# Group 0's output projection and first norm in one range of 512 tokens, with gMLP's last gate unit and two head units behind them

## The chip, the core and the metric

The kernel runs on one core of a Trainium2 chip. Its engines work side by side, each through its own queue in order: TensorE (PE, matmuls; its weight loads are PEld), VectorE (DVE), ScalarE (ACT), GpSimd (POOL) and SyncE (SP), which here issues nearly all DMAs. The metric is the device time of one execution in microseconds (us), as the median of several runs. Where several kernels are compared, less is better.

## The reference

One layer of a streaming encoder, for a prompt of 1024 tokens and a sample of 32 tokens of a running stream, with the same weights (`D_MODEL` 1024, `D_FF` 2816, all in float32):

```python
sh1, sc1, g1, sh2, sc2, g2 = jnp.split((jax.nn.silu(c) @ w_ada + b_ada)[:, None, :], 6, axis=-1)
h = x * (1 + sc1) + sh1
mq, mk, mv, mo, mi, mf, fq, fk, fv, ff, gu, gv = jnp.split(h @ w_in, split_at, axis=-1)
hm = ...   # mLSTM, chunk by chunk
hf = ...   # forgetting attention (FoX), causal
vn = _layer_norm(gv, gmlp_ln_g, gmlp_ln_b)
hg = _spatial_gate(gu, vn, gmlp_ws, gmlp_bs)      # gMLP, in chunks of 128 tokens
mix = jnp.concatenate([hm, hf, hg], axis=-1) @ w_o
x = _layer_norm(ALPHA * x + (1 + g1) * mix, ln1_g, ln1_b)
h = x * (1 + sc2) + sh2
y = (jax.nn.silu(h @ w_gate) * (h @ w_up)) @ w_down
x = _layer_norm(ALPHA * x + (1 + g2) * y, ln2_g, ln2_b)
```

## The kernel before

**Layout.** Features lie on the 128 partitions (KT = 8 blocks of 128), tokens along the free dimension. The 1056 tokens are two groups: group 0 is tokens 0 to 511, group 1 the other 512 and the 32 of the sample (544). Tokens are also counted in 9 tiles: 0 to 3 are group 0, 4 to 7 and the sample tile 8 are group 1. `MM[0]` cuts group 0 into ranges of 256 tokens, `MM[1]` group 1 into ranges of 272; `WIDE` is group 0 in one range of 512.

**Products.** Each float32 product is made of three matmuls of rounded parts (`gemm`, L117 to L119): an operand x is split into a high part (a cast, on ScalarE) and the rest (a subtraction, on VectorE). `weights` loads a weight block of 512 KB into one of three buffers (`raw`), casts it (L105) and splits it (L106). An operand's buffers are `hh` and `hl`.

**Order.** The program is written in an order, but each instruction is placed by a scheduler that simulates the engines; the queues that result are fixed. Memory pools are stacks: a pool that is opened gets the room of one that was closed, and what is written into it waits for the last readers of the old tiles.

**The stage of the change**, in the order in which it is written in `run`:

- The mixers of group 0, `fox` (heads q0 to q7) and `mlstm` (four chunks), with high priority; in their pauses other units' matmuls run. Their outputs go to HBM (`dmix[0]`, eight blocks of 128 rows).
- `wo_res(0)` loads the residual x into `z[0]` (8 loads of 256 KB); `wo_mix(0, ...)` brings `dmix[0]` back, a block and a range of 256 tokens at a time, through four buffers `tmp`, and splits it (L919, L920): first blocks 2, 3, 4, 5, 0, 1 (`KORDER[:6]`) for the one range, then for the other; blocks 6 and 7 (gMLP's) at its second call.
- Four gMLP units (`tm_unit`): 0 and 2 make `gv` with its norm (`evac_gv`) for tiles 0 to 3 and 4 to 8, 1 and 3 make `gu` and the gate (`evac_gmlp`) for the same tiles. A tile is 24 matmuls (L282 to L284, for the sample tile L287 to L290); `evac_gmlp` adds a load of `gvn`, a copy on ScalarE (L644), eight small products (L649), four VectorE operations (L652), transposes (L631), a copy (L633) and a store to `dmix`.
- `fm_unit` for heads 2 and 3, group 1 only: 48 matmuls each; evacuation on ScalarE (L366), VectorE (L367) and GpSimd (L368, into `o_kT`), with three stores per range.
- `wo(0, ...)` for the first and then for the second range of 256: for each of 8 output blocks m it loads `w_o[m]`, makes 24 matmuls, adds the residual (L960), subtracts a pivot (L955, GpSimd; the pivot is the mean of block 0), and sums z (L860, GpSimd) and its squares (L856, L862). For m = 0 the matmuls go by operand block, as these arrive.
- `ln1(0, ...)` for each range: means by matmuls with ones (L872), reciprocal root (L879 to L883), then for each block a multiplication (L977), an addition (L978, for two of eight blocks on GpSimd), an affine step on ScalarE (L981) and the split (L985, L986) into the buffers that the projection's operand had.
- `fm_unit` for heads 4 to 7, and `ln1_res(0)`, GpSimd's 16 operations on z (L995).
- The mixers of group 1, at high priority, over the SwiGLU units `up(0, j)` and `down(0, g)` of group 0. Unit j = 0 runs in two ranges of 256, the others in one of 512; behind each of the first four stands one conditioning unit (`ada`, L179).

PSUM has eight banks; `pg`, from which the gMLP units, heads and the projection take theirs, has three of them.

Of the kernel before, what the change touches and what calls it, by code (L numbers as in the profile page):

```python
# [7 lines left out]
F32 = mybir.dt.float32  # L8
F32R = mybir.dt.float32r
AF = mybir.ActivationFunctionType  # L10
ALU = mybir.AluOpType
# [58 lines left out]
class Kernel:  # L70
# [769 lines left out]

    def ln_pivot(self, st, z, sl):
        nc = self.nc
        ps = self.t(self.pt, [P, 512], F32, "t")
        n = sl.stop - sl.start
        nc.tensor.matmul(ps[:, :n], self.ones8, z[:, 0, sl], start=True, stop=True)
        nc.scalar.copy(st["pv"][:, sl], ps[:, :n])
        nc.vector.tensor_tensor(z[:, 0, sl], z[:, 0, sl], st["pv"][:, sl], ALU.subtract)

    def ln_sum(self, st, z, m, sl):
# [5 lines left out]
        sq = self.t(self.p2, [P, 272], F32, "tmp", 4)[:, :sl.stop - sl.start]  # L855
# [29 lines left out]
    def ln_stats(self, st, sl):  # L885
# [3 lines left out]
        v = self.t(self.p2, [P, 272], F32, "tmp", 4)[:, :sl.stop - sl.start]  # L889
# [61 lines left out]
    def sublayer_end(self, c, z, m, ps, gate, st, a, b):  # L951
# [3 lines left out]
        less = lambda: self.nc.gpsimd.tensor_tensor(z[:, m, sl], z[:, m, sl], st["pv"][:, sl], ALU.subtract)  # L955
# [13 lines left out]
    def ln1(self, c, st, a, b):  # L969
# [3 lines left out]
        for k in range(KT):  # L973
# [4 lines left out]
            (nc.gpsimd if k % 4 == 1 else nc.vector).tensor_tensor(zk, zk, e, ALU.add)  # L978
            h = self.t(self.p2, [P, 272], F32, "tmp", 4)[:, :b - a]
# [250 lines left out]
    def run(self):  # L1230
# [114 lines left out]
        for i in range(4):  # L1345
            if i == ADAPOS:
                tail_ada()
            self.tm_unit(w2[3 + i % 2], 256, (self.evac_gv, self.evac_gmlp)[i % 2], range(4 * (i // 2), 4 + i // 2 * 5),
                         nc.gpsimd if GENG[i] else nc.vector)
        if ADAPOS == 4:  # L1350
            tail_ada()
        for h in range(QD, PRE):
            self.fm_unit(w3[2 + h], self.evac_qk(h), (1,))
        s6.close()
        self.wo_mix(0, self.KORDER[6:])
        self.pn = self.pool("pn")
        self.ln_consts()
        st = self.ln_begin(nc.gpsimd)
        for cut in MM[0]:
            self.wo(0, st, (cut,), nc.vector)  # L1360
        self.operand(0, self.ph)
        for a, b in MM[0]:
            weave(self.ln1(0, st, a, b))
        for h in range(PRE, 8):
            self.fm_unit(w3[2 + h], self.evac_qk(h), (1,))
        self.ln1_res(0)
# [10 lines left out]
        for g, (j0, nj) in enumerate(GROUPS):  # L1377
# [26 lines left out]
            for j in range(j0 + (g > 0), j0 + nj + (g < last)):  # L1404
                weave(self.up(0, j, act, pa, WIDE if 0 < j < GROUPS[-1][0] else MM[0]))
                if j < 4:
                    self.ada(20 + j, self.wp, "raw", RAW, self.pg, "g")
# [165 lines left out]
```

## Time and profile before

| | |
|---|---|
| median of 3 runs | 1400.97 us (1399.07 to 1403.76) |
| span of the profiled execution, first to last instruction | 1388.5 us |
| between the span and the median of the runs | 12.5 us |
| PE / DVE / ACT / POOL busy | 97% / 74% / 46% / 19% |
| mean granted TensorE clock | 0.993 |

The time of the profiled execution itself is not among the runs; its span is what the stage rows add up to. Where a row shows an engine's instructions, its name is followed by the source line (L106), the operation, and output and inputs by the program's names. A tile's name begins with the phase in which it was made: `tm_` belongs to the gMLP units, `fm_` to heads, `wo_` to the projection, `lna_` to the first norm, `up_` to the SwiGLU units. `mlstm_ah` and `mlstm_al` are the operand buffers `hh[0]` and `hl[0]`, and `mlstm_z` is `z[0]`. A matmul's duration reaches past the start of the next one; its cost in a stream is the distance from start to start.

### The profile page before, as it was taken

The page shows a single profiled execution, that of the slowest core. Times are in us where ns is not written, and L with a number is a line of the kernel's source. Part 1 is how long each engine was busy: PE and PEld are TensorE (multiplying, and loading weights), DVE is VectorE, ACT ScalarE, POOL GpSimd, SP SyncE. Part 2 cuts the span into 40 slices and gives each one's busy share as a digit, 9 for nine tenths or more (in the row PEclk, how much of TensorE's full clock was granted, in tenths as well). Part 3 has the DMA queues.
Part 4 walks back from the last instruction along what each step waited for, and adds up shares of the span by engine and source line. Part 5 has one row for each costly group of instructions (what it writes and reads, how often), then busy time and mean ns, then how long its engine had stood idle before and what let it go on. Part 6 is the DMA issues. An engine that isn't in the chain of part 4 may idle for free.

```text
span 1388.5 us, 25995 instructions
## 1 busy us (share of the span) xinstructions
PE 1345.2 (97%) x9683; PEld 1236.4 (89%) x9683; DVE 1034.2 (74%) x2214; ACT 641.3 (46%) x1261; POOL 259.1 (19%) x292
## 2 busy tenths in 40 slices
PE   7999999999999799999999999999999999999996
PEld 4899988899899778888887889899999999999996
DVE  5548656678689657777776766677898988888777
ACT  3323234444455444545544445335574544545355
POOL 0103200052157500000000000264610000000341
PEclk9999999999999899999999999999999999999998
DMA  9754577575665665444443442664497767453321
GB/s 362 266 211 134 176 242 212 187 237 149 212 205 160 180 184 182 125 131 137 133 135 86 108 127 81 195 169 134 157 229 195 216 163 214 136 175 115 101 90 65
DMA packets 136373, 233.09 MB, mean 168 GB/s; under 512 B 22564, under 2 KB 79532, under 8 KB 136248
## 3 DMA queue, kind: packets, MB, share of 16 engines
q1 hardware_dynamic: 130936, 221.34, 50.7%
q0 software_dynamic: 5168, 9.96, 4.7%
q8 instruction: 76, 1.25, 0.4%
q14 instruction: 49, 0.40, 0.1%
q10 hardware_dynamic: 144, 0.14, 0.0%
HBM read 197.50 MB, written 53.81 MB: 181 GB/s over the span
## 4 chain that ended last, share of the span: by engine, by line
PE 67%; DVE 5%; DMA 3%; ACT 1%; issue 1%; SPq 0%; POOL 0%; DVEq 0%; ACTq 0%
PE up_g L117 5%; PE up_g L118 5%; PE up_g L119 5%; PE dn_g L119 4%; PE dn_g L117 4%; PE dn_g L118 4%; PE sup_u L119 3%; PE sup_u L117 3%; PE sup_u L118 3%; PE wo_g L119 2%; PE wo_g L117 2%; PE wo_g L118 2%; PE sup_g L118 2%; PE sup_g L119 2%; PE sup_g L117 2%; PE fox_t L738 2%
## 5 line engine op out<-in xcount | busy, mean ns | idle before, releaser
L117 PE MATMUL up_g<-mlstm_ah,up_whi 128*128 128x512 f32 (+1 forms) x384 | 141.7, 369 | 4.4 <-ACT lna_tmp L981 3.3
L118 PE MATMUL up_g<-mlstm_al,up_whi 128*128 128x512 f32 (+1 forms) x384 | 142.1, 370 | 0.4 <-DVE mlstm_al L986 0.4
L119 PE MATMUL up_g<-mlstm_ah,up_wlo 128*128 128x512 f32 (+1 forms) x384 | 141.1, 368 | 0.0
L282 PE MATMUL tm_g<-tm_whi,start_h1h 128*128 128x256 f32 (+1 forms) x384 | 109.7, 287 | 1.5 <-ACT tm_mixs L633 1.5
L284 PE MATMUL tm_g<-tm_whi,start_h1l 128*128 128x256 f32 (+1 forms) x384 | 109.6, 287 | 0.0
L283 PE MATMUL tm_g<-tm_wlo,start_h1h 128*128 128x256 f32 (+1 forms) x384 | 109.5, 286 | 0.0
L117 PE MATMUL fm_g<-start_h1h,fm_whi 128*128 128x256 f32 (+2 forms) x344 | 101.7, 301 | 6.1 <-DVE fm_qkl L367 2.6
L118 PE MATMUL fm_g<-start_h1l,fm_whi 128*128 128x256 f32 (+2 forms) x344 | 100.8, 293 | 0.0
L119 PE MATMUL fm_g<-start_h1h,fm_wlo 128*128 128x256 f32 (+2 forms) x344 | 100.0, 292 | 0.0
L1105 ACT CAST sup_whi<-sup_raw 128x1024 fp32r<-128x1024 f32 x54 | 56.0, 1048 | 91.5 <-PE dn_u L118 47.9
L117 PEld LDWEIGHTS up_g<-mlstm_ah,up_whi 128*128 128x128 f32 x384 | 73.5, 192 | 16.7 <-ACT mlstm_ah L985 3.5
L118 PEld LDWEIGHTS up_g<-mlstm_al,up_whi 128*128 128x128 f32 x384 | 73.7, 192 | 12.3 <-DVE mlstm_al L986 1.5
L119 PEld LDWEIGHTS up_g<-mlstm_ah,up_wlo 128*128 128x128 f32 x384 | 73.8, 192 | 10.6
L105 ACT CAST up_whi<-up_raw 128x1024 fp32r<-128x1024 f32 x50 | 52.4, 1048 | 63.9 <-PE dn_g L118 25.1
L711 ACT ACTIVATE fox_p<-fox_s,fox_fmx 128x384 f32<-128x384 f32 (+2 forms) x96 | 55.0, 578 | 57.1 <-DVE fox_fmx L709 44.0
L282 PEld LDWEIGHTS tm_g<-tm_whi,start_h1h 128*128 128x128 f32 x384 | 72.2, 189 | 4.4 <-ACT tm_mixs L633 2.1
L117 PEld LDWEIGHTS fm_g<-start_h1h,fm_whi 128*128 128x128 f32 x344 | 64.7, 190 | 12.5 <-DVE fm_qkl L367 3.5
L1106 DVE TENSOR_TENSOR sup_wlo<-sup_raw,sup_whi 128x1024 fp32r<-128x1024 f32 x54 | 67.8, 1259 | 10.5 <-ACT sup_whi L1105 10.5
L106 DVE TENSOR_TENSOR up_wlo<-up_raw,up_whi 128x1024 fp32r<-128x1024 f32 x50 | 66.8, 1336 | 10.4 <-ACT up_whi L105 9.6
L284 PEld LDWEIGHTS tm_g<-tm_whi,start_h1l 128*128 128x128 f32 x384 | 72.2, 188 | 1.5 <-issue 1.2
L117 PE MATMUL dn_g<-up_acth,dn_whi 128*128 128x512 f32 (+2 forms) x200 | 73.5, 368 | 0.0
L118 PE MATMUL dn_g<-up_actl,dn_whi 128*128 128x512 f32 (+2 forms) x200 | 73.3, 368 | 0.0
(591 smaller groups left out, 4594.5 us busy)
## 6 DMA issues: line engine op xcount, KB each, us to landing
up_raw<-w_gu SPq DMA_DIRECT2D x50, 512.0 KB
dn_raw<-w_dn SPq DMA_DIRECT2D x28, 512.0 KB
ada_late<-w_ada SPq DMA_DIRECT2D x24, 512.0 KB
wo_raw<-w_o SPq DMA_DIRECT2D x24, 512.0 KB
sup_raw<-w_gu SPq DMA_DIRECT2D x20, 512.0 KB
start_dp<-w_gu SPq DMA_DIRECT2D x19, 512.0 KB
start_dp<-w_gu POOLq DMA_DIRECT2D x19, 512.0 KB, 7.8
sup_raw<-start_dp SPq DMA_DIRECT2D x18, 512.0 KB
```

The source lines that it names most:

```text
L105: nc.scalar.copy(hi[:, :w], raw[:, :w])
L106: (eng or nc.vector).tensor_tensor(lo[:, :w], raw[:, :w], f(hi[:, :w]), ALU.subtract)
L117: nc.tensor.matmul(ps, hi, xh(k), start=start and k == 0, stop=False)
L118: nc.tensor.matmul(ps, hi, xl(k), start=False, stop=False)
L119: nc.tensor.matmul(ps, lo, xh(k), start=False, stop=stop and k == n - 1)
L282: nc.tensor.matmul(ps[:, :ncol], xh, hi, start=k == 0, stop=False)
L283: nc.tensor.matmul(ps[:, :ncol], xh, lo, start=False, stop=False)
L284: nc.tensor.matmul(ps[:, :ncol], xl, hi, start=False, stop=k == 7)
L711: nc.scalar.activation(pr[:, lo:hi], banks[x][:, :hi - lo], AF.Exp, bias=mxs[:, 0:1], accum_out=sums[:, x:x + 1])
L738: nc.tensor.transpose(ps[:, c:c + P], probs[y][:, b * P:(b + 1) * P], self.ident)
L1105: nc.scalar.copy(h, x)
L1106: tt(l, x, f(h), ALU.subtract)
```

## The change

Group 0's projection takes one range of 512 tokens, so w_o is loaded and split once, in place of twice. In this range the pivot's subtraction and the sum of z go to VectorE (`st["eng"]` is `nc.vector`; group 1 keeps GpSimd), and so do the two additions of the norm that GpSimd had. Buffers of 512 columns come from a pool `pw` (`ltmp`). gMLP's unit 3 and heads 2 and 3 are written behind the norm. The conditioning units 20 to 23 go from the first SwiGLU units to heads 4 to 7, and SwiGLU unit 0 takes one range of 512. `wo_mix` still loads by ranges of 256.

```diff
+    def ltmp(self, n):
+        if n > 272:
+            return self.t(self.pw, [P, 512], F32, "wide", 4)[:, :n]
+        return self.t(self.p2, [P, 272], F32, "tmp", 4)[:, :n]
...
-        sq = self.t(self.p2, [P, 272], F32, "tmp", 4)[:, :sl.stop - sl.start]
+        sq = self.ltmp(sl.stop - sl.start)
...
-        v = self.t(self.p2, [P, 272], F32, "tmp", 4)[:, :sl.stop - sl.start]
+        v = self.ltmp(sl.stop - sl.start)
...
-        less = lambda: self.nc.gpsimd.tensor_tensor(z[:, m, sl], z[:, m, sl], st["pv"][:, sl], ALU.subtract)
+        less = lambda: (self.nc.gpsimd if c else st["eng"]).tensor_tensor(z[:, m, sl], z[:, m, sl], st["pv"][:, sl],
+                                                                          ALU.subtract)
...
-            (nc.gpsimd if k % 4 == 1 else nc.vector).tensor_tensor(zk, zk, e, ALU.add)
-            h = self.t(self.p2, [P, 272], F32, "tmp", 4)[:, :b - a]
+            (nc.gpsimd if c and k % 4 == 1 else nc.vector).tensor_tensor(zk, zk, e, ALU.add)
+            h = self.ltmp(b - a)
...
-        for i in range(4):
-            if i == ADAPOS:
-                tail_ada()
-            self.tm_unit(w2[3 + i % 2], 256, (self.evac_gv, self.evac_gmlp)[i % 2], range(4 * (i // 2), 4 + i // 2 * 5),
-                         nc.gpsimd if GENG[i] else nc.vector)
-        if ADAPOS == 4:
-            tail_ada()
-        for h in range(QD, PRE):
-            self.fm_unit(w3[2 + h], self.evac_qk(h), (1,))
+        gate = lambda i: self.tm_unit(w2[3 + i % 2], 256, (self.evac_gv, self.evac_gmlp)[i % 2],
+                                      range(4 * (i // 2), 4 + i // 2 * 5), nc.gpsimd if GENG[i] else nc.vector)
+        for i in range(3):
+            gate(i)
+        tail_ada()
         s6.close()
         self.wo_mix(0, self.KORDER[6:])
         self.pn = self.pool("pn")
+        sw = ExitStack()
+        self.pw = self.pool("pw", ctx=sw)
         self.ln_consts()
-        st = self.ln_begin(nc.gpsimd)
-        for cut in MM[0]:
-            self.wo(0, st, (cut,), nc.vector)
-        self.operand(0, self.ph)
-        for a, b in MM[0]:
-            weave(self.ln1(0, st, a, b))
-        for h in range(PRE, 8):
+        st = self.ln_begin(nc.vector)
+        self.wo(0, st, WIDE, nc.vector)
+        weave(self.ln1(0, st, *WIDE[0]))
+        gate(3)
+        for h in range(QD, 8):
             self.fm_unit(w3[2 + h], self.evac_qk(h), (1,))
+            if h >= PRE:
+                self.ada(16 + h, self.wp, "raw", RAW, self.pg, "g")
+        sw.close()
         self.ln1_res(0)
...
-                weave(self.up(0, j, act, pa, WIDE if 0 < j < GROUPS[-1][0] else MM[0]))
-                if j < 4:
-                    self.ada(20 + j, self.wp, "raw", RAW, self.pg, "g")
+                weave(self.up(0, j, act, pa, WIDE if j < GROUPS[-1][0] else MM[0]))
```

## The prediction

> **What bounds the kernel now.** I read the page first, then busy time by stage, then the waits of the stage that the change touches, then single instructions there.
>
> ```profile
> span 1388.5 us, 25995 instructions
> PE 1345.2 (97%) x9683; PEld 1236.4 (89%) x9683; DVE 1034.2 (74%) x2214; ACT 641.3 (46%) x1261; POOL 259.1 (19%) x292
> 346.90:361.50 14.60, 14.60 (x129) 13.39 (x127) 13.69 (x48) 5.62 (x14) 5.11 (x4) 1.00 0.38 113
> 361.50:384.70 23.20, 20.87 (x169) 19.87 (x168) 13.03 (x34) 11.61 (x27) 1.93 (x3) 1.00 0.86 269
> 384.70:433.80 49.10, 47.37 (x392) 46.88 (x391) 42.67 (x53) 24.54 (x39) 33.04 (x30) 1.00 0.63 197
> 433.80:461.10 27.30, 26.38 (x201) 25.52 (x200) 21.77 (x42) 15.78 (x34) 16.57 (x19) 1.00 0.48 149
> 461.10:488.00 26.90, 20.55 (x129) 18.21 (x130) 20.80 (x53) 12.83 (x30) 12.76 (x19) 0.81 0.72 197
> 482.00:536.00 54.00, 53.66 (x340) 41.55 (x340) 32.03 (x79) 26.57 (x58) 0.95 (x1) 0.99 0.65 192
> 536.00:700.00 164.00, 164.00 (x854) 137.89 (x851) 126.97 (x275) 81.55 (x163) 4.56 (x9) 1.00 0.47 140
> ```
>
> Columns of the stage rows: stretch, length, then busy time of TensorE matmul, TensorE weight load, VectorE, ScalarE, GpSimd, then granted clock. TensorE sets the end (97%); from 482 on it never pauses, so what it loses or gains before that reaches the end one for one. The prediction is a ledger of TensorE's lost time between 346.9 and the SwiGLU units at 461-488.
>
> Losses now: 0 + 2.33 + 1.73 + 0.92 + 6.35 = 11.3 us. The 6.35 are mostly the norm and a bank that is late, and the clock halves behind those pauses:
>
> ```profile
> PE up_g L117 <- ACT lna_tmp L981: 3.3, 1, 3.3
> PE ada_g L179 <- DVE up_sil L1037: 2.3, 1, 2.3
> 465.00:470.00 5.00, 2.08 (x18) 1.87 (x16) 5.00 (x11) 3.68 (x8) 2.61 (x3) 0.93 0.17 60
> 470.00:475.00 5.00, 4.22 (x18) 3.96 (x19) 2.90 (x8) 5.00 (x14) 5.00 (x9) 0.50 0.48 146
> 475.00:480.00 5.00, 2.69 (x26) 1.90 (x25) 3.89 (x10) 0.61 (x2) 2.11 (x5) 0.84 0.88 217
> 480.00:485.00 5.00, 5.00 (x36) 4.45 (x28) 2.40 (x8) 0.95 (x2) 0.00 (x0) 0.71 1.16 246
> ```
>
> At half clock half the busy time is lost: 4.22/2 in the second row, about 0.75 in the third (1.6 us halved), 1.45 in the fourth (2.9 us halved): 4.3 us. Before: 15.6 us in all. That is the most that a better cover of the norm can return.
>
> **What the change saves in matmuls.** The projection goes from 384 matmuls of 256 columns to 192 of 512. Start to start:
>
> ```profile
> 462.26 0.28 PE L117 MATMUL up_g<-mlstm_ah,up_whi 128*128 128x256 f32 x1
> 462.38 0.28 PE L118 MATMUL up_g<-mlstm_al,up_whi 128*128 128x256 f32 x1
> 560.98 0.39 PE L118 MATMUL up_g<-mlstm_al,up_whi 128*128 128x512 f32 x1
> 561.21 0.39 PE L119 MATMUL up_g<-mlstm_ah,up_wlo 128*128 128x512 f32 x1
> ```
>
> 0.12 against 0.23 us (0.119 and 0.2335 over longer runs): 45.7 against 44.8 us, 0.9 saved; unit 0's 96 into 48 save another 0.2. Half of the weight loads, casts and splits of w_o fall away (8 each); they already run beside matmuls, so nothing. The four conditioning units (ada) that go from the first SwiGLU units into heads 4 to 7 are the same matmuls elsewhere; their loads share three weight buffers with the heads, whose 6 us of matmuls cover a load of 2.1, its cast and its split (1.2, L106 below): nothing.
>
> **What it uncovers ahead of the projection.** Up to the last matmul of gate unit 2 both instruction orders are alike. Behind it TensorE now runs gate unit 3 and heads 2 and 3; in the changed order only the remains of the mixers stand there, then the projection. The projection cannot start then. Its operand comes through HBM, issued in order on SP's queue:
>
> ```profile
> 346.76 0.28 PE L288 MATMUL tm_g<-tm_whi,start_hs 128*64 128x256 f32 x1
> 359.55 0.43 DVE L621 TENSOR_TENSOR mlstm_mhm<-mlstm_mhm,mlstm_mo 128x256 f32<-128x256 f32 x1
> 360.96 0.38 SPq L91 DMA_DIRECT2D start_dmix<-mlstm_mixs  x1
> 362.56 3.75 SPq L87 DMA_DIRECT2D mlstm_z<-xT  x8
> 366.35 2.37 SPq L87 DMA_DIRECT2D wo_tmp<-start_dmix  x4
> 372.46 2.41 SPq L87 DMA_DIRECT2D wo_tmp<-start_dmix  x4
> 371.57 1.50 ACT L919 CAST mlstm_ah<-wo_tmp 128x256 fp32r<-128x256 f32 x4 [1.20 <-DMA wo_tmp<-start_dmix]
> 379.63 1.75 SPq L87 DMA_DIRECT2D wo_tmp<-start_dmix  x4
> 382.28 0.41 ACT L919 CAST mlstm_ah<-wo_tmp 128x256 fp32r<-128x256 f32 x1 [0.16 <-DMA wo_tmp<-start_dmix]
> ```
>
> The mixers' last store leaves at 361. It follows L621, and the stretch 346.9-361.5 has VectorE busy 13.69 of 14.60: VectorE sets it. In the changed order VectorE has the same work there (two weight splits of w_o replace the two of gate and head), so I leave the store at 361. Behind it on SP, as now, come eight loads of x (2 MB) and the 16 loads of the mixers' output through four buffers; the first casts come 9.0 us after the first x load (362.56 to 371.57). With nothing between, later groups of four need a free buffer (cast 0.4, split 0.4), issue and landing: 2.1 us uncontended (379.63 to 381.7), some 3.1 in all. Loading still goes by 256-token halves, but a 512-wide matmul needs both, and the first row block of the second half is load 7: cast at 375.5. Bounds: 372.5 if every landing is short; 378.5 if the second group lands as late as today (372.46 to 378.74).
>
> Gate 3's and the heads' own loads and stores, which today stand among these on SP, are behind them now; that is already in the 3.1.
>
> ```profile
> 346.90:384.70 37.80, 20.32 (x164) 18.62 (x162) 5.53 (x23) 3.78 (x11) 1.00 0.68 209
> 346.90:384.70 37.80, 12.63 (x95) 12.16 (x96) 1.00 (x2) 1.45 (x3) 1.00 0.68 209
> ```
>
> These are the same stretch for the gate's matmuls (tm_g) and the heads' (fm_g) alone: 20.3 + 12.6 = 33 us with overlapping ends, some 31.5 without. 35.5 us were busy there in all, so 4.0 of mixer work stay. 346.9 to 375.5 is 28.6 us; lost: **24.6 us** (21.6 to 27.6). This is the term that decides.
>
> After it the projection runs behind at half clock, as after the pause at 467-470 (6.8 us halved there): I take 2.0 us (0 to 3.4), since part of it coincides with waiting for the last loads.
>
> [...]
>
> **What the norm does to its new cover.** Behind the projection stand gate unit 3, heads 2 to 7: 31.5 + 24 us of TensorE work, longer than the norm. But gate 3's evacuation is on VectorE too (L652), queued between the norm's instructions, and TensorE has three PSUM banks. Durations:
>
> ```profile
> L554 DVE TENSOR_TENSOR mlstm_mw<-mlstm_s,mlstm_mw x9: 269/691/692, 264.9 to 759.0; 128x512 f32<-128x512 f32 x8, 32x128 f32<-32x128 f32 x1
> L977 DVE TENSOR_TENSOR mlstm_z<-mlstm_z,wo_pv x16: 410/414/970, 440.8 to 466.4; 128x256 f32<-128x256 f32 x16
> L106 DVE TENSOR_TENSOR wo_wlo<-wo_raw,wo_whi x24: 1203/1226/2097, 370.6 to 934.5; 128x1024 fp32r<-128x1024 f32 x24
> L652 DVE SCALAR_TENSOR_TENSOR tm_traw<-tm_g,start_colp,tm_traw x36: 262/274/285, 314.2 to 375.9; 128x64 f32<-128x64 f32 x32, 32x64 f32<-32x64 f32 x4
> L872 PE MATMUL lna_t<-wo_zs,start_onesm x8: 377/384/392, 433.6 to 974.7; 128*128 128x256 f32 x4, 128*128 128x272 f32 x4
> L649 PE MATMUL tm_g<-tm_gvn,start_wsp x72: 214/275/281, 313.1 to 375.0; 128*128 128x64 f32 x64, 32*32 32x64 f32 x8
> L960 DVE SCALAR_TENSOR_TENSOR mlstm_z<-dn_g,start_mod,mlstm_z x48: 467/750/755, 541.8 to 997.2; 128x512 f32<-128x512 f32 x40, 128x256 f32<-128x256 f32 x8
> L862 DVE TENSOR_TENSOR wo_qs<-wo_qs,wo_tmp x28: 428/954/2120, 401.3 to 953.6; 128x256 f32<-128x256 f32 x14, 128x272 f32<-128x272 f32 x14
> ```
>
> A 512-wide VectorE operation lies between the 256- and the 1024-wide rows, near L554: 0.69 busy, 0.60 start to start as neighbours overlap. Within the projection VectorE needs 0.75 + 1.2 + 2 x 0.6 = 3.2 us for a block of 5.6 us matmuls: hidden, and no longer doubled by GpSimd (L862: 0.43 to 2.12). The seven pivot subtractions that it takes from GpSimd come in one piece behind the first block, 4.2 us, while two more blocks are being multiplied: hidden too; without that cover they would hold the next bank for 4.2 us.
>
> From the projection's end (0), down both queues. VectorE: last block, sum, a weight split, sum of squares, 3.1. TensorE takes the two means between gate matmuls, 0.43 for each 256 columns (two L872 that overlap), and is through with them at 7.6. Variance 8.3, logarithm and exponential on ScalarE 9.7, three VectorE steps to the reciprocal root 11.6, half of the second tile's L652 and the shift 13.3, eight multiplications 18.1, the other half 18.6. TensorE has by then 96 matmuls (11.4), the means (1.7), one pair of transposes (0.25) and three times eight small products (2.5; L649 at 0.1 start to start) behind it, and wants that tile's transposes at 15.9: 2.7 lost. It goes on with the sample tile (24 matmuls, 2.9) and 1.1 of products and transposes, and at 22.8 wants those of the fourth tile, all banks full; its L652 stand on VectorE behind the third tile's, eight additions, three operand splits and a weight split: 28.6, 5.8 lost. **8.5 us** (0 if the evacuations get through as they do today; 12.5 if GpSimd's ln1_res, which runs beside the additions, slows VectorE as in L862's upper half). Another pause, another half clock: 1.5 us (0 to 3.4). The last splits end at some 35 us, before the heads do; the SwiGLU units find their operand ready, so the two waits at 461-488 go.
>
> **Sum.** After: 24.6 + 2.0 + 8.5 + 1.5 = 36.6. Before: 15.6. Matmuls -1.1. 36.6 - 15.6 - 1.1 = **+19.9 us**: span 1408.4. The runs lie at 1400.97 where the profiled span is 1388.5, 12.5 outside it; the forecast is **1421**. Extremes: 21.6 - 16.7 = +5; 27.6 + 3.4 + 12.5 + 3.4 - 16.7 = +30. Its own range 1412 to 1428.
>
> **Rivals.**
> 1. *Only the hole ahead of the projection.* VectorE serves gate 3 in time. For it: today VectorE is busy only 21.77 of 27.30 in 433-461. Against it: an in-order queue with eight operations ahead of L652. 24.6 + 2.0 - 16.7 = +10: 1411.
> 2. *Not slower: TensorE's own queue holds the mixers' tail.* Of the 14.60 us busy in 346.9-361.5, 10.6 are filler that stands ahead of the mixers' matmuls. If that made the tail late, dropping it brings the store, and all of SP's chain, 10.6 us forward; the hole shrinks to 14.0, and with the evacuations in time and the clock kept: 14.0 - 16.7 = -3: 1398. It decides from a first projection matmul before 367.6. Against it: VectorE's 13.69 of 14.60, and 9 us of loads that stay.
> 3. *Worse behind the norm.* GpSimd has all 16 ln1_res ahead of the first head's o_kT addition, whose stores stand on SP ahead of later weight loads.
>
> ```profile
> L995 POOL TENSOR_SCALAR mlstm_z<-mlstm_z,start_colp x16: 550/822/1768, 445.8 to 476.6; 128x256 f32<-128x256 f32 x16
> ```
>
>  If the second eight take 1.77 us each instead of 0.55, the heads wait some 10 us more: +30, 1431.
> 4. That the change does nothing is excluded by the built order: 8735 rows of TensorE instructions against 8977, and the moved units behind the norm.
>
> **Chances.** Forecast 0.56, rival 1 0.20, rival 2 0.08, rival 3 0.13, rest 0.03. 1407 to 1431 takes in rivals 1 and 3 and leaves out rival 2. No change that can be told here means within 0.3% (4.2 us): rival 2 mostly falls there or just below. Faster 0.05, same 0.06, slower 0.89.
>
> **What would show it.** Right: TensorE idle for some 14 us without break up to about 375, released by a cast of the mixers' output; the projection ending some 10 us earlier than 433.8 all the same; two pauses of 3 and 6 us ahead of gate 3's transposes, released by its L652 on VectorE; granted clock 0.5 behind each; no wait for the norm at the first SwiGLU unit. Wrong: a mixers' store well before 361, a first projection matmul before 368, or no VectorE-released pauses behind the projection.

## The result and the profile after

| | before | after |
|---|---|---|
| median of 4 runs | 1400.64 us (1399.07 to 1403.76) | 1433.05 us (1431.06 to 1434.53) |
| ratio, 95% interval | | 1.0247 (1.0225 to 1.027) |
| span of the profiled execution | 1388.5 us | 1429.0 us, in a run of 1431.06 |

The change costs 32.4 us. The forecast was 1421, its range ended at 1431. Slower was right, and so was the hole in which most of the time goes; 12 us more were lost than the sum had.

The stages of the kernel after: stretch, length, busy time of TensorE matmul, TensorE weight load, VectorE, ScalarE, GpSimd, then granted clock.

```profile
span 1429.0 us, 25316 instructions
PE 1355.0 (95%) x9437; PEld 1232.4 (86%) x9437; DVE 1022.2 (72%) x2176; ACT 628.9 (44%) x1221; POOL 225.1 (16%) x260
...
354.63:383.30 28.67, 6.00 (x39) 3.42 (x37) 14.99 (x51) 7.58 (x19) 5.05 (x4) 0.61 0.52 167
383.30:388.40 5.10, 5.09 (x12) 4.03 (x13) 2.74 (x7) 2.43 (x6) 0.00 (x0) 0.50 0.60 175
388.40:431.40 43.00, 43.00 (x184) 34.28 (x184) 26.99 (x38) 13.43 (x19) 0.00 (x0) 1.00 0.29 88
431.40:508.60 77.20, 67.20 (x525) 61.11 (x523) 39.54 (x83) 28.70 (x53) 28.60 (x32) 0.93 0.47 146
508.60:538.60 30.00, 28.98 (x139) 22.86 (x142) 19.03 (x33) 13.52 (x20) 2.44 (x6) 1.00 0.82 232
540.00:800.00 260.00, 260.00 (x1347) 217.48 (x1346) 184.75 (x394) 124.67 (x249) 4.76 (x11) 1.00 0.46 125
800.00:820.00 20.00, 17.86 (x77) 13.70 (x76) 13.85 (x26) 9.04 (x20) 0.72 (x1) 0.91 0.49 112
820.00:925.00 105.00, 105.00 (x601) 90.00 (x600) 75.32 (x155) 49.83 (x102) 0.00 (x0) 1.00 0.39 104
925.00:955.00 30.00, 26.11 (x185) 24.33 (x184) 20.82 (x30) 12.81 (x31) 16.91 (x15) 0.94 0.64 199
```

The first row begins behind the last matmul of gate unit 2 and ends with the projection's first: 28.67 us, of which TensorE works 6.00. The second is the projection's beginning at half clock, the fourth gate unit 3 and the heads behind the norm. The two rows behind 800 are new: in the kernel before, TensorE lost 0.7 us between 540 us and the end of group 1's projection.

What TensorE waited for in the kernel after (total, times, longest) between 340 and 560 us:

```profile
PE wo_g L117 <- ACT mlstm_ah L924: 14.2, 1, 14.2
PE tm_g L631 <- DVE tm_traw L652: 6.1, 2, 3.4
PE mlstm_t L631 <- DVE mlstm_mhm L621: 6.0, 1, 6.0
PE mlstm_t L560 <- DVE fox_ptl L744: 1.7, 1, 1.7
...
PE fm_g L119 <- DVE fm_wlo L106: 1.0, 2, 0.7
PE tm_g L288 <- ACT tm_mixs L633: 1.0, 1, 1.0
PE up_g L117 <- ACT up_whi L105: 1.0, 1, 1.0
PE fm_g L117 <- ACT fm_whi L105: 0.9, 1, 0.9
```

The same view between 560 and 1000 us, whole:

```profile
PE fox_s L702 <- ACT fox_p L711: 2.1, 1, 2.1
PE wo_g L117 <- ACT up_ah L924: 2.0, 2, 1.7
PE wo_g L118 <- DVE up_al L925: 1.4, 2, 0.8
PE wo_g L117 <- DMA wo_raw<-w_o: 0.5, 1, 0.5
```

The first hole is three waits in a row (1.7, 6.0, 14.2). The second view holds two more holes. Its first row is a wait of the mixers themselves, at 801.6: TensorE wants the next scores of `fox`, ScalarE is late with an exponential (L711), and that stands in ScalarE's queue behind a gate of the mLSTM (L538), which waited for its load:

```profile
801.23 0.42 ACT L538 ACTIVATE mlstm_mo<-mlstm_mo 32x256 f32<-32x256 f32 x1 [6.41 <-DMA mlstm_mo<-start_dmo]
```

In the kernel before, the same operation waited 4.76 us, and TensorE 0.5. The other three rows are the second hole proper, with `up_ah` and `up_al` the operand of *group 1's* projection. Its cause shows in one view: the last matmuls of the mixers of group 1 (L751) and the first of group 1's projection (L117), with count, durations, first and last start. First the kernel before, then after:

```profile
L751 PE MATMUL fox_o<-fox_pth,fox_v x112: 272/280/287, 530.0 to 874.8; 128*128 128x256 f32 x96, 128*128 128x128 f32 x16
L117 PE MATMUL wo_g<-up_ah,wo_whi x128: 282/287/487, 901.8 to 950.4; 128*128 128x272 f32 x128
```

```profile
L751 PE MATMUL fox_o<-fox_pth,fox_v x112: 272/280/288, 573.8 to 924.9; 128*128 128x256 f32 x96, 128*128 128x128 f32 x16
L117 PE MATMUL wo_g<-up_ah,wo_whi x128: 282/287/486, 935.6 to 991.1; 128*128 128x272 f32 x128
```

Between the two lay 27.0 us of SwiGLU matmuls; now there are 10.7. In these the last mixer output must be stored, loaded and split, and that takes longer. In the order as built, 160 SwiGLU matmuls stood there and now 84. (These matmuls of the mixers begin 44 us later and end 50 us later, the projection begins 34 us later.)

### The profile page after: what moved, and what is told of

The parts are those of the page before. It is cut to its first block, busy times and chain, and to the rows that moved or that the text cites. A ratio compares the mean times of both kernels' runs of the same rounds, so it can differ in the third digit from the quotient of the medians.

```text
span 1429.0 us, 25316 instructions
## 1 busy us (share of the span) xinstructions
PE 1355.0 (95%) x9437; PEld 1232.4 (86%) x9437; DVE 1022.2 (72%) x2176; ACT 628.9 (44%) x1221; POOL 225.1 (16%) x260
## 4 chain that ended last, share of the span: by engine, by line
PE 60%; DVE 7%; DMA 5%; issue 3%; ACT 1%; SPq 0%; POOL 0%; DVEq 0%; ACTq 0%; POOLq 0%
PE up_g L117 5%; PE up_g L118 5%; PE up_g L119 5%; PE dn_g L119 3%; PE dn_g L117 3%; PE dn_g L118 3%; PE sup_u L119 3%; PE sup_u L117 3%; PE sup_u L118 3%; PE wo_g L117 2%; PE wo_g L118 2%; PE wo_g L119 2%; PE sup_g L119 2%; PE sup_g L118 2%; PE sup_g L117 2%
## 5 line engine op out<-in xcount | busy, mean ns | idle before, releaser
L117 PE MATMUL up_g<-mlstm_ah,up_whi 128*128 128x512 f32 (+1 forms) x368 | 138.0, 375 | 1.0 <-ACT up_whi L105 1.0
L119 PE MATMUL up_g<-mlstm_ah,up_wlo 128*128 128x512 f32 (+1 forms) x368 | 137.6, 374 | 0.5 <-DVE up_wlo L106 0.5
L118 PE MATMUL up_g<-mlstm_al,up_whi 128*128 128x512 f32 (+1 forms) x368 | 137.2, 373 | 0.0
L117 PE MATMUL fm_g<-start_h1h,fm_whi 128*128 128x256 f32 (+2 forms) x344 | 102.6, 303 | 6.8 <-ACT fm_whi L105 2.8
L117 PEld LDWEIGHTS up_g<-mlstm_ah,up_whi 128*128 128x128 f32 x368 | 69.2, 188 | 13.3 <-ACT up_whi L105 1.4
L119 PEld LDWEIGHTS up_g<-mlstm_ah,up_wlo 128*128 128x128 f32 x368 | 69.2, 188 | 12.9 <-DVE up_wlo L106 1.0
L711 ACT ACTIVATE fox_p<-fox_s,fox_fmx 128x384 f32<-128x384 f32 (+2 forms) x96 | 55.2, 580 | 56.3 <-DVE fox_fmx L709 43.4
L118 PEld LDWEIGHTS up_g<-mlstm_al,up_whi 128*128 128x128 f32 x368 | 69.2, 188 | 11.6
L117 PEld LDWEIGHTS fm_g<-start_h1h,fm_whi 128*128 128x128 f32 x344 | 66.0, 194 | 13.7 <-ACT fm_whi L105 4.3
L1112 DVE TENSOR_TENSOR sup_wlo<-sup_raw,sup_whi 128x1024 fp32r<-128x1024 f32 x54 | 67.9, 1261 | 10.5 <-ACT sup_whi L1111 10.5
L743 ACT CAST fox_pth<-fox_t 128x512 fp32r<-128x512 f32 (+1 forms) x80 | 40.9, 544 | 76.4 <-PE fox_t L738 76.2
L117 PE MATMUL dn_g<-up_acth,dn_whi 128*128 128x512 f32 (+2 forms) x200 | 74.3, 372 | 0.0
L283 PEld LDWEIGHTS tm_g<-tm_wlo,start_h1h 128*128 128x128 f32 x384 | 73.4, 191 | 0.7 <-issue 0.4
L119 PE MATMUL dn_g<-up_acth,dn_wlo 128*128 128x512 f32 (+2 forms) x200 | 73.7, 368 | 0.0
```

Source lines behind the costliest of these rows:

```text
L117: nc.tensor.matmul(ps, hi, xh(k), start=start and k == 0, stop=False)
L118: nc.tensor.matmul(ps, hi, xl(k), start=False, stop=False)
L119: nc.tensor.matmul(ps, lo, xh(k), start=False, stop=stop and k == n - 1)
L283: nc.tensor.matmul(ps[:, :ncol], xh, lo, start=False, stop=False)
L711: nc.scalar.activation(pr[:, lo:hi], banks[x][:, :hi - lo], AF.Exp, bias=mxs[:, 0:1], accum_out=sums[:, x:x + 1])
L743: nc.scalar.copy(ph[:, :e], ps[:, :e])
```

## The experiments

"Lost" is TensorE's idle time and what half clock cost, added over stretches of 1 us: length less busy time, and busy time times (1 - clock). It is given for three places. A: from 50 us ahead of group 0's projection to 15 us into it. B: from that projection's end to 30 us into the first SwiGLU unit. C: from there to 5 us behind the end of group 1's projection. The part of C that lies between the mixers' last matmul and the end of that projection has a column of its own, "at wo". "Cover" is the number of SwiGLU matmuls that the build puts between the last mixer matmul and group 1's projection. Ratios are to runs of the kernel before on the same chip, whose medians were 1394.5 to 1395.4 us (1400.6 for the kernel after); the times in the expectations start from 1400.6, so ratios are what is compared.

| kernel | ratio (95%) | A | B | C | at wo | cover |
|---|---|---|---|---|---|---|
| before, first profile | | 4.7 | 11.6 | 0.7 | 0.0 | 160 |
| e0, before again | | 4.1 | 12.3 | 0.8 | 0.0 | 160 |
| after | 1.0247 (1.0225 to 1.027) | 27.3 | 15.2 | 9.4 | 5.6 | 84 |
| e1 | 1.0056 (1.0031 to 1.0081) | 3.0 | 15.8 | 11.0 | 5.1 | 83 |
| e2 | 1.0159 (1.0129 to 1.0188) | 25.0 | 4.8 | 8.5 | 2.2 | 105 |
| e4 | 1.0221 (1.0202 to 1.0241) | 27.8 | 12.0 | 9.9 | 6.8 | 48 |
| e6 | 1.02 (1.0173 to 1.0226) | 21.4 | 19.2 | 8.8 | 3.4 | 83 |
| e7 | 1.025 (1.0219 to 1.0281) | 27.6 | 14.9 | 6.6 | 1.5 | 179 |
| e8 | 1.0068 (1.0042 to 1.0095) | 2.6 | 13.2 | 11.1 | 2.8 | 105 |
| e9 | 1.0005 (0.9986 to 1.0025) | 2.8 | 14.0 | 1.3 | 0.0 | 159 |
| e10 | 1.0237 (1.0203 to 1.027) | 27.4 | 16.3 | 8.6 | 5.4 | 83 |
| e19 | 1.0218 (1.0188 to 1.0247) | 21.4 | 20.8 | 10.8 | 5.6 | 83 |
| e20 | 1.0066 (1.004 to 1.0092) | 8.8 | 14.0 | 7.8 | 3.0 | 105 |
| e21 | 1.0037 (1.0023 to 1.0051) | 4.9 | 9.2 | 6.9 | 3.0 | 83 |

(In B, what e2, e19 and e20 lost inside group 0's projection is included. A difference of one in the last column means nothing: the traces have the same number there for after, e1, e6, e10, e19 and e21, and for before, e0 and e9.)

**e0: the kernel before, profiled again.** No edit.

> The kernel before, unedited, for a second profile. Theory: the profiled span of 1388.5 us was an unusually quick execution, not the usual one with 12.5 us outside it. Then this profile has a span near 1398, about 2 us outside the span as the kernel after has (1431.06 beside 1429.0), and TensorE loses some 26 us before 342 us, as the kernel after does (26.9), where the first profile has 18.7. Rival: the change itself slows the first 342 us, though no instruction there differs. Then the span is 1388 to 1391 again and the loss there 18 to 20 us.

Run 1395.83 us, span 1393.8: 2.0 outside the span, not 12.5. The first 340 us held these busy times (TensorE first) in e0, and the first 342 in the first profile:

```profile
0.00:340.00 340.00, 317.64 (x2569) 287.02 (x2569) 213.58 (x595) 119.91 (x281) 54.17 (x81) 0.99 0.68 219
```

```profile
0.00:342.00 342.00, 323.35 (x2617) 292.16 (x2618) 219.71 (x619) 121.75 (x288) 57.95 (x85) 1.00 0.68 219
```

Idle 22.4 against 18.7 us with the same kernel. The clock differs too: in these first 342 us half clock cost nothing in the first profile, 1.6 us in e0 and 4.8 in the kernel after. The span is not quite the 1398 expected but 5 us above the first. Ahead of A, the kernels here lost between 18 and 26 us in no order that their edits would explain. So some 8 of the 40.5 us between the two profiled spans are this spread, and the rest is 32.

**e1: gate unit 3 and heads 2 and 3 back ahead of the projection.**

```diff
-        for i in range(3):
+        for i in range(4):
             gate(i)
         tail_ada()
+        for h in range(QD, PRE):
+            self.fm_unit(w3[2 + h], self.evac_qk(h), (1,))
...
-        gate(3)
-        for h in range(QD, 8):
+        for h in range(PRE, 8):
```

> The kernel after, with gMLP's last gate unit and heads 2 and 3 back ahead of the projection; one range of 512 tokens, VectorE alone and the moved conditioning units stay. Theory: two holes make up the loss, one ahead of group 0's projection (25.7 us more lost between 342 and 540 than before) and a second one ahead of group 1's projection (8.6 us more lost after 740), because the mixers of group 1 end 10.7 us ahead of that projection where it was 27.0. In this kernel's build 83 SwiGLU matmuls stand between the mixers' last matmul and group 1's projection, as after (84), not 160 as before, so only the first hole closes: 1433 - 26 = 1407 us, 1403 to 1411. Rival A, the move is all of it: 1399, 1397 to 1401. Rival B, the single range on VectorE alone costs by itself as well: over 1412.

1.0056, on the theory's 1.005. The first hole is gone (A 3.0), the second one is as it was; its group 1's rows:

```profile
L751 PE MATMUL fox_o<-fox_pth,fox_v x112: 272/280/287, 546.0 to 897.2; 128*128 128x256 f32 x96, 128*128 128x128 f32 x16
L117 PE MATMUL wo_g<-up_ah,wo_whi x128: 282/287/486, 908.0 to 963.0; 128*128 128x272 f32 x128
```

10.8 us from 897.2 to 908.0, as after. So the moved units open the first hole, and something else in the change opens the second and lengthens the mixers' own wait (2.6 us at 773.7 here).

**e2: only the move, on the kernel before.**

```diff
-        for i in range(4):
+        for i in range(3):
...
-        for h in range(QD, PRE):
-            self.fm_unit(w3[2 + h], self.evac_qk(h), (1,))
...
-        for h in range(PRE, 8):
+        gate(3)
+        for h in range(QD, 8):
```

> The kernel before, with only gMLP's last gate unit and heads 2 and 3 moved behind the norm; two ranges of 256, GpSimd's part and the conditioning units in the SwiGLU loop stay. Theory: the first hole is the move's, so it is here too, the idle time ahead of the projection 20 to 28 us. In this build 105 SwiGLU matmuls stand behind the mixers' last one, between before (160) and after (84), so the second hole is half there, 2 to 6 us. Together 1401 + 24 + 4 = 1429, 1422 to 1434. Rival A, the loss comes from the single range and VectorE: 1400 to 1410. Rival B, no second hole: below 1422.

1.0159, 22 us: at the lower edge. A is 25.0, so the hole is the move's. The surprise is B, 4.8 us where before has 12 and after 15: with two ranges of 256 the moved units cover the norm, and the move gets 7 us back. Of C's 8.5 only 2.2 lie at group 1's projection; 2.2 are the mixers' wait for ScalarE, 2.2 one for a load (`fox_qp`), and most of the rest is half clock.

**e4: heads 2 to 7 ahead of gate unit 3, behind the norm.**

```diff
-        gate(3)
         for h in range(QD, 8):
...
+        gate(3)
         sw.close()
```

> The kernel after, with heads 2 to 7 ahead of gMLP's last gate unit behind the norm instead of behind it. Theory of the second hole: in this build only 48 SwiGLU matmuls (5.8 us) stand between the mixers' last matmul and group 1's projection, against 84 (10.7 us) after, so TensorE waits some 5 us more there: idle time between the last mixer matmul and 30 us into group 1's projection of 8 to 10 us against 3.9, and 1438 in all, 1434 to 1442, unless the gate unit's two stalls of 7.1 us behind the projection go (up to 7 less, read apart from the profile). Rival, the wait there isn't set by that cover: 3 to 5 us of it again.

1.0221 where 1.024 was the least expected: a miss. C is 9.9, and of the idle time at group 1's projection 3.7 us remain, not 8 to 10, with a cover of 48. The idle time does not grow as the cover shrinks from 84 to 48; with half clock the loss there grows from 5.6 to 6.8. The count alone does not give its size.

**e7: one more SwiGLU unit ahead of group 1's projection.**

```diff
                 weave(self.up(0, j0 + 1, act, pa, MM[0]))
+                weave(self.up(0, j0 + 2, act, pa, MM[0]))
...
-                    for j in range(j0 + 2, j0 + nj):
+                    for j in range(j0 + 3, j0 + nj):
```

> The kernel after, with one more SwiGLU unit of group 0 (unit 20, 96 matmuls, some 11.5 us) issued ahead of group 1's projection and taken from the fill of group 1's norm. Theory of the second hole: TensorE waits there because too little work stands between the mixers' last store and that projection; with 179 SwiGLU matmuls there, not 84, the 5.6 us lost between the mixers' last matmul and the projection's end (3.9 idle, 1.7 at half clock) go to under 1, and nothing comes back behind it, since a unit and the down products still cover the norm. Ratio to before 1.0247 - 0.004 = 1.0207 (1.018 to 1.023). Rival: what is late there is late for another reason (the loads of the mix in SP's queue, the casts behind SwiGLU on ScalarE), so 3 us or more stay, or come back in group 1's norm, and the ratio is 1.024 or more.

1.025: nothing gained, the rival's outcome. From the mixers' last matmul to the projection's end TensorE lost 1.5 us, not 5.6, so the wait there was one for cover. (The mixers' wait for ScalarE stayed: 1.8 us and 1.7 at half clock.) But 3.5 us came back behind it (0.3 after), where TensorE now waits in group 1's norm and for a unit's weights (kernel e7, waits behind 940 us):

```profile
PE up_g L118 <- DVE wo_al L992: 1.5, 2, 1.0
PE up_u L117 <- ACT up_whi L105: 1.4, 1, 1.4
```

**e6: heads 2 and 3 alone ahead of the projection.**

```diff
         tail_ada()
+        for h in range(QD, PRE):
+            self.fm_unit(w3[2 + h], self.evac_qk(h), (1,))
...
-        for h in range(QD, 8):
+        for h in range(PRE, 8):
```

> The kernel after, with only heads 2 and 3 (10.5 us of matmuls) back ahead of the projection; the gate unit stays behind the norm. Theory: the first hole is the mix's own trip (store, 24 loads, casts), which lasts as long whatever TensorE does in it, so each microsecond of work put there shortens it one for one: the loss from 50 us ahead of the projection to 15 us into it falls from 27.2 us to 16 to 18. The second hole stays. Ratio to before 1.0247 - 0.0075 = 1.017 (1.0145 to 1.0195). Rival: the heads' own weight loads and casts hold the mix's trip up, or the heads wait themselves, so the loss falls by less than 6 us and the ratio is over 1.020.

1.020, between the two. 10.5 us of matmuls shortened A by 5.9 us only. The DMA issues of SP in e6 say why in part:

```profile
370.21 0.37 SPq L91 DMA_DIRECT2D start_dmix<-mlstm_mixs  x1
370.67 0.45 SPq L87 DMA_DIRECT2D wo_raw<-w_o  x1
371.21 0.40 SPq L91 DMA_DIRECT2D start_dql<-fm_qkl  x1
371.70 4.38 SPq L87 DMA_DIRECT2D mlstm_z<-xT  x8
376.36 2.29 SPq L87 DMA_DIRECT2D wo_tmp<-start_dmix  x4
379.05 0.48 SPq L91 DMA_DIRECT2D o_kT<-fm_qkr  x1
382.37 7.90 SPq L87 DMA_DIRECT2D wo_tmp<-start_dmix  x12
```

A load of `w_o` and a store of a head's result stand between the mixers' store and the loads of x, and the first load of the mix leaves 6.2 us behind that store, against 4.4 after (369.53 to 373.88). The other store of a head's result, between the fourth and the fifth load of the mix, costs next to nothing: in both kernels the fifth load waits for a buffer and leaves 0.9 us behind the first cast. The projection's first matmul is at 385.90, 15.7 us behind the mixers' last store, against 13.8 after; and the store itself leaves 23.1 us behind the last chunk's first transposes (347.08), against 20.0 after (349.53). Together that is 5.0 of the 10.5 us; what delays the store is not shown. So here cover that has loads and stores of its own on the queue did not shorten the hole one for one.

**e19: the loads of x behind those of the mix.**

```diff
-        self.wo_res(0, self.pz)
         self.operand(0, self.ph)
...
         self.wo_mix(0, self.KORDER[6:])
+        self.wo_res(0, self.pz)
```

> The kernel after, with the eight loads of x for group 0's residual written behind the loads of the mix; in this build two of them stand behind the fourth of the mix's loads and three each behind the eighth and twelfth. Theory of the first hole: it is the trip of the mix through SP's queue; from the mixers' last store (369.53) to the first matmul of the projection (383.31) it takes 13.8 us, 3.9 of them the eight loads of x. Without them ahead the trip takes 9.5 to 11.5 us, the loss from 50 us ahead of the projection to 15 us into it falls from 27.2 to 23 to 25, and the ratio to before is 1.0247 - 0.0022 = 1.0225. Rival: the landing of the stored mix or the casts set the trip, and the loads of x lie in their shadow: 13 us or more, no change.

1.0218, as the theory's 1.0225, though the interval would not tell it from after. In its trace the loads of the mix follow the store at once, and the first matmul follows at 375.63, 8.0 us behind the store, less than expected:

```profile
367.59 0.39 SPq L91 DMA_DIRECT2D start_dmix<-mlstm_mixs  x1
368.07 1.85 SPq L87 DMA_DIRECT2D wo_tmp<-start_dmix  x4
369.98 0.90 SPq L87 DMA_DIRECT2D wo_z<-xT  x2
371.49 2.18 SPq L87 DMA_DIRECT2D wo_tmp<-start_dmix  x4
```

A fell by 5.8 us; B rose by as much (half clock 7.6 us there, 4.2 after), so nearly all of it was given back in this profile.

**e10: GpSimd's part of the norm given back.**

```diff
-        st = self.ln_begin(nc.vector)
+        st = self.ln_begin(nc.gpsimd)
         self.wo(0, st, WIDE, nc.vector)
...
-            (nc.gpsimd if c and k % 4 == 1 else nc.vector).tensor_tensor(zk, zk, e, ALU.add)
+            (nc.gpsimd if k % 4 == 1 else nc.vector).tensor_tensor(zk, zk, e, ALU.add)
```

> The kernel after, with GpSimd's part in the norm given back (sum of the statistics, pivot's subtraction, every fourth addition), one range of 512 and the move stay. After's gate unit pauses 7.1 us behind the projection for its VectorE casts, and the stretch from the projection's end to 30 us into SwiGLU loses 15.2 us, where the move with two ranges and GpSimd lost 3.5. Theory V, VectorE alone is the cause: the stretch loses 5 to 9 us and the ratio to before is 1.0247 - 0.005 = 1.0195 (1.017 to 1.022). Theory R, the single range is: its statistics end once for 512 tokens and VectorE then has the whole norm in one block, so the stretch loses 13 to 18 us and the ratio is 1.0235 to 1.028.

1.0237, B 16.3: theory R, though the interval of the ratio reaches into V's. The gate unit waits as long as after (5.3 us for L652 and 2.0 for a transposed copy; after 6.1 and 1.0), where in e2, with two ranges, it waited 1.8 us for L652. So the loss of GpSimd's help is not what holds up the evacuation.

**e9: only the range and VectorE, on the kernel before.** It is e1 with the conditioning units back in the SwiGLU loop and unit 0 in two ranges; the diff is to e1.

```diff
-            if h >= PRE:
-                self.ada(16 + h, self.wp, "raw", RAW, self.pg, "g")
...
-                weave(self.up(0, j, act, pa, WIDE if j < GROUPS[-1][0] else MM[0]))
+                weave(self.up(0, j, act, pa, WIDE if 0 < j < GROUPS[-1][0] else MM[0]))
+                if j < 4:
+                    self.ada(20 + j, self.wp, "raw", RAW, self.pg, "g")
```

> The kernel before, with only group 0's projection and norm in one range of 512 tokens on VectorE alone; the gate unit and heads 2 and 3 stand ahead of the projection, the conditioning units in the SwiGLU loop, SwiGLU unit 0 in two ranges, all as before. In this build 159 SwiGLU matmuls stand behind the mixers' last one, as before. Theory: both holes belong to the moves (gate unit and heads: first hole; conditioning units and unit 0: half of the second), so both are closed: what is left is 1.1 us of matmuls saved and some 0 to 4 us more of waits of heads 4 to 7 behind a norm that VectorE does alone. Ratio to before 1.001, 0.998 to 1.004. Rival: the range and VectorE cost 8 us or more by themselves, as e1's loss of 15.8 us behind the projection suggests: 1.005 or more.

1.0005 (0.9986 to 1.0025): the part that the change is named for neither costs nor saves anything that can be told. With cover 159, C is 1.3.

**e8: e9 with SwiGLU unit 0 in one range.** The diff to e9 is the one condition `0 < j` taken out.

> e1 with the four conditioning units back in the SwiGLU loop; only SwiGLU unit 0 in one range tells it from e9. In this build 105 SwiGLU matmuls stand behind the mixers' last one (83 in e1, 159 in e9). Behind 700 us TensorE lost 9.3 us up to the end of group 1's projection in e1 (ratio 1.0056) and 1.0 in e9 (1.0005). Theory: the second hole is set by how far the mixers lag behind SwiGLU in the built order, and both small edits push them back, so this kernel lies between: 3 to 7 us lost there, ratio 1.003 (1.001 to 1.0045). Rival, the conditioning units alone did it: under 2 us lost, ratio 1.0005. Rival, unit 0's range alone did it: 8 us or more, ratio 1.0056.

1.0068, C 11.1 of which 6.4 lie behind 700 us, 2.8 of them at group 1's projection and 3.7 at the mixers' wait for ScalarE. By time it is the rival in which unit 0's range does it alone; by loss behind 700 it lies between. The cover fell from 159 to 105 by that edit.

**e21: the conditioning units alone, on the kernel before.**

```diff
         for h in range(PRE, 8):
             self.fm_unit(w3[2 + h], self.evac_qk(h), (1,))
+            self.ada(16 + h, self.wp, "raw", RAW, self.pg, "g")
...
-                if j < 4:
-                    self.ada(20 + j, self.wp, "raw", RAW, self.pg, "g")
```

> The kernel before, with one edit: the four conditioning units stand behind heads 4 to 7, not behind the first four SwiGLU units. The prediction costed this part of the change at nothing. In this build 83 SwiGLU matmuls stand behind the mixers' last one, not 159, as in the kernel after. Theory: that alone opens the second hole; TensorE loses 8 to 11 us from 700 us to the end of group 1's projection, where before loses 0.8, and nothing ahead of group 0's projection (4 us, as before). Where the units cover part of the norm's wait, the stretch behind group 0's projection loses up to 4 us less than 12.3. Ratio to before 1.005 (1.002 to 1.008). Rival, as predicted: the same matmuls in another place of a saturated TensorE, under 2 us lost behind 700 us, ratio 0.997 to 1.001.

1.0037 (1.0023 to 1.0051), in the theory's interval and outside the rival's. A is unchanged (4.9), B lost 3.1 less, C 6.2 more: 2.7 up to 700, 4.2 behind it, half of what was expected there. The 2.7 are a wait for a load (`foxs_k`, 1.0) and a stretch at half clock; of the 4.2, 3.0 lie at group 1's projection. Its rows:

```profile
L751 PE MATMUL fox_o<-fox_pth,fox_v x112: 272/280/287, 544.8 to 893.7; 128*128 128x256 f32 x96, 128*128 128x128 f32 x16
L117 PE MATMUL wo_g<-up_ah,wo_whi x128: 282/287/491, 904.5 to 957.6; 128*128 128x272 f32 x128
```

Again 10.8 us of cover. The units cover some of the norm's wait, and the kernel pays for it later.

**e20: heads 2 and 3 behind the norm, gate unit 3 ahead of the projection, loads of x late; on the kernel before.** An attempt to win at B without losing at A.

```diff
-        self.wo_res(0, self.pz)
...
-        for h in range(QD, PRE):
-            self.fm_unit(w3[2 + h], self.evac_qk(h), (1,))
         s6.close()
         self.wo_mix(0, self.KORDER[6:])
+        self.wo_res(0, self.pz)
...
-        for h in range(PRE, 8):
+        for h in range(QD, 8):
```

> The kernel before, with heads 2 and 3 alone moved behind the norm, the gate unit kept ahead of the projection, and the loads of x behind the mix's: some 24 us of the gate unit's matmuls cover the mix's trip, and 10.5 us of heads cover the norm. Theory: the stretch from the projection's end to 30 us into SwiGLU loses 3 to 5 us, not 12.3 (the move with two ranges lost 3.5 there); the first hole opens by no more than 4 us, since the trip is shorter by the loads of x; the build leaves 105 SwiGLU matmuls behind the mixers' last one, so up to 8 us are lost behind 500 us as in the move alone. Together -8 + 2 + 6: ratio 1.000, 0.995 to 1.004. Rival, the second hole isn't tied to that count: it stays closed, ratio 0.995 or less. Rival, the first hole needs the heads as well: ratio 1.006 or more.

1.0066: the last rival. A opened to 8.8 us and 3.9 more were lost inside the projection, so the gate unit alone is too little cover; C is 7.8. No kernel here beats the one before.

## Why the prediction was right in kind and short in size

The ledger, term by term, in us; "after" from the rows above.

| term | predicted | measured |
|---|---|---|
| hole ahead of the projection | 24.6 | 23.6 |
| half clock behind it | 2.0 | 2.6 |
| stalls behind the projection | 8.5 | 10.0 |
| half clock with them | 1.5 | 4.2 |
| waits at the first SwiGLU units | 0 | 1.0 |
| mixers' wait for ScalarE, with half clock | 0 | 3.8 |
| second hole, at group 1's projection, with half clock | 0 | 5.6 |
| sum after | 36.6 | 50.8 |
| less before | 15.6 | 16.4 |
| matmuls | -1.1 | -1.7 |
| **change** | **+19.9** | **+32.7** |

The hole is 28.67 - 6.00 = 22.7 idle and 1.0 at half clock; behind it, 5.10 us at 0.50; the stalls are 77.20 - 67.20; the mixers' wait is 2.1 idle and 1.7 at half clock at 800 us, the second hole 3.9 and 1.7. "Before" has its 0.7 behind 700 added; -1.7 is the difference of the two spans less all that each lost. Behind 1000 us 0.4 less is lost, which makes 32.3, and the medians show 32.4. The loss ahead of gate unit 2's end is left out; e0 shows it to be spread.

1. *The hole* was right in place, releaser and size: 28.67 us from gate unit 2's end to the projection, 28.6 predicted, released by a cast of the mixers' output after 14.2 us without a break. e1 and e2 show that the move opens it, e19 that the loads of x are part of it. Rival 2 fell: the mixers' store left at 369.53, or 361.8 less the 7.7 us that this execution was late by then, where 361 was predicted. Its two halves were off by less than a microsecond each, and these cancelled: the store left 14.9 us behind gate unit 2's end, not 14.1, and the projection began 13.8 us behind the store, not 14.5. 6.0 us of mixer work stood there, not 4.0, and 1.0 of it was half clock, which makes 23.6 of the 24.6.
2. *The projection ending early* was right: 431.4, 2.4 earlier than before, 10.1 without the 7.7.
3. *The pauses of gate unit 3* came where predicted, 2.6 and 3.4 us for 2.7 and 5.8, both released by L652. The transposes in the trace of the kernel after, with the idle time ahead of them:

```profile
450.22 0.69 PE L631 MATMUL tm_g<-start_ident,tm_traw 128*128 128x128 f32 x2 [2.64 <-DVE tm_traw L652]
451.92 0.48 PE L288 MATMUL tm_g<-tm_whi,start_hs 128*64 128x256 f32 x1 [1.01 <-ACT tm_mixs L633]
460.60 0.69 PE L631 MATMUL tm_g<-start_ident,tm_traw 128*128 128x128 f32 x2 [3.42 <-DVE tm_traw L652]
```

   What was mis-sized is the clock (4.2 for 1.5, since half clock came with each pause, 6.82 us from 449.87 and 3.41 from 460.11) and what follows: the heads waited some 3 us, 1.9 of them for casts and splits of weights (L105, L106), and the first units 1.0, which the sum had at nothing. The loads behind these waits took 5.2, 5.2 and 6.7 us from issue (483.89, 493.27 and 500.84) to landing, where the prediction counted 2.1; each stands on the queue behind a load of a conditioning unit, which the prediction counted at nothing, but that this made them late is not tested. As for the pauses ahead of the transposes, e10 rules out the loss of GpSimd's help as their reason; the single range is what is left, and with two ranges (e2) the same wait for L652 was 1.8 us.
4. *Rival 3* fell. GpSimd's 16 `ln1_res` did run ahead of the heads' additions (451.7 to 469.9), and they held a store of `o_kT` on SP for 3.1 us; but TensorE waited for nothing between 461 and 491.
5. **The step that failed** is the one at the very beginning, "from 482 on it never pauses, so what it loses or gains before that reaches the end one for one", and with it the costing of the conditioning units: "the same matmuls elsewhere ... nothing". A saturated TensorE hid that the mixers of group 1 had 27.0 us of cover ahead of the next projection. The change takes that down to 10.7, and the second projection then meets the same trip of its operand through HBM that the first one met: 5.6 us. Another 3.8 are lost at 801, where TensorE's wait for ScalarE grew from 0.5 to 2.1 us and 3.4 us at half clock followed. e21 shows the hole at the projection with the conditioning units alone (3.0), e8 against e9 with unit 0's range alone (2.8 and 0.0), e9 without either. The built order, which the prediction used for the first stage, had the 84 matmuls for 160 in it; it was not read that far.
6. *The base* was right for a wrong reason. "12.5 outside" the span was no such thing; a run lies 2.0 outside its own span (e0, after), and the first profile was simply a short execution. The +19.9 were set against the runs' median all the same.

What stays open is why the scheduler puts the mixers so much later for such small edits. The cover takes the values 159, 105, 83 and 48 in these builds; the edits do not add up (conditioning units alone 83; with unit 0's range and the units left in the loop 105), and the loss in C does not follow the count closely. The part of it at group 1's projection does follow in order: 0.0 with 159 and 160 matmuls, 2.2 to 3.0 with 105, 3.0 to 5.6 with 83 and 84, 6.8 with 48; only e7 (1.5 with 179) is out of it. The rest of C is waits of the mixers for loads and for ScalarE, and half clock. The wait for ScalarE follows another one: where the gate's load kept ScalarE for 4.8, 5.3, 6.0, 6.4 and 6.9 us (before, e21, e7, after, e1), TensorE waited 0.5, 1.0, 1.8, 2.1 and 2.6. Why the load lands later in the edited kernels is open.

## What to carry to other kernels

Work that is moved away from ahead of a transfer chain (store, load, split) uncovers the whole chain, and it is found by putting the chain's own issues, from the store to the first matmul, beside the work that is left there. Where an engine is saturated, look for the next chain that its work covers, and compare in the new order how much work stands between that chain's end and its reader: a saturated stretch is no proof that what happens in it is free. Before using one profiled span as the base of a sum, put it beside the run it belongs to.

## What the runs showed of the hardware

In the kernel after, half clock followed a pause of 2.1 us, and it came after work had resumed. TensorE idles 2.14 us up to 803.7 at a granted clock of 1.00, and 0.50 is granted from 804.9 to 808.3:

```profile
800.00:804.00 4.00, 1.86 (x9) 1.23 (x7) 1.01 (x2) 2.72 (x8) 0.00 (x0) 1.00 0.67 40
804.90:808.30 3.40, 3.40 (x11) 2.43 (x10) 3.40 (x6) 1.33 (x2) 0.32 (x1) 0.50 0.82 249
```

So this wait cost 2.1 + 1.7 us. The sum had 3.5 us of half clock (2.0 and 1.5); measured are 1.0 + 2.6 + 4.2 + 3.4 = 11.2. In the kernel after, the four stretches at half clock between 440 and 1000 us last 6.82, 3.41, 3.42 and 3.41 us (from 449.87, 460.11, 804.85 and 951.63).

The length of the pause alone does not decide. A pause of 2.71 us in e0 (200.43 to 203.13) is longer than the one at 803.7, and the clock stays at 1.00:

```profile
198.40:201.81 3.41, 2.03 (x18) 1.83 (x16) 1.13 (x4) 0.81 (x3) 0.00 (x0) 1.00 0.72 212
201.81:205.23 3.42, 2.10 (x18) 2.13 (x19) 0.74 (x2) 0.97 (x2) 0.00 (x0) 1.00 0.49 162
205.23:208.64 3.41, 3.41 (x32) 3.07 (x31) 2.29 (x9) 1.94 (x7) 0.00 (x0) 1.00 0.12 40
```

In e10 half clock follows where TensorE shows no idle time at all but runs 24 matmuls of 32 columns (L829):

```profile
557.06:560.47 3.41, 3.41 (x31) 2.76 (x31) 1.37 (x3) 0.92 (x3) 0.00 (x0) 1.00 0.46 154
560.47:563.88 3.41, 3.41 (x10) 2.63 (x9) 1.84 (x6) 1.23 (x4) 0.00 (x0) 0.50 0.60 163
```

In the kernel after, the same 24 matmuls run from 557.47 to 559.84, and the clock stays at 1.00. So a short pause cost 1.7 us of half clock in one place and nothing in another, and what decides is not shown; the half clock of the first 342 us (0, 1.6 and 4.8 us in three executions, see e0) is part of the spread between runs.

The other is the spread: with no edit at all, ten runs of the kernel before beside e1, e2 and e4 went from 1389.6 to 1400.36 us. A difference of 0.3% needs several runs on both sides.
